# Two-layer decoder trunk on one core: causal mask added by VectorE with the row maximum, ACT issuing the stores of what it wrote, and first scores in single PSUM banks

## Chip, core and metric

The kernel runs on one core of one Trainium2 chip. The metric is the device time of one execution in microseconds (us), less is better. The core has a matrix engine (TensorE, PE in the profile; its weight loads are listed apart as PEld), a vector engine (VectorE, DVE), a scalar engine (ScalarE, ACT), GpSimd (POOL) and SyncE (SP), which here issues most DMA transfers. Each engine works through its own instructions in order and waits on semaphores of the others. Matmuls write to PSUM (eight banks of 2 KB for each of 128 partitions), everything else lives in SBUF.

## The reference

An input of 1024 tokens x 1024 features, all in fp32, passes two layers. Layer 0 is a matrix-memory LSTM (mLSTM) followed by an MLP; then keys and values are computed once from the residual stream; layer 1 is attention with its own low-rank query path, then another MLP. What matters here is layer 1's attention: 8 heads, each with 128 plain and 64 rotated query/key columns, causal.

```python
def causal_mla_attention(q_nope, q_rope, k_nope, k_rope, v):
    ...
    scale = (B_NOPE + B_ROPE) ** -0.5
    ...
        s = (jnp.einsum('bqhd,bkhd->bhqk', qn_b, k_nope)
             + jnp.einsum('bqhd,bkd->bhqk', qr_b, k_rope)).astype(jnp.float32) * scale
        qpos = start + jnp.arange(B_QBLOCK, dtype=jnp.int32)
        s = jnp.where(kpos[None, :] <= qpos[:, None], s, -jnp.inf)
        p = jax.nn.softmax(s, axis=-1)
        return jnp.einsum('bhqk,bkhd->bqhd', p.astype(v.dtype), v)
...
def sqrelu_mlp(h, w1, w2):
    return jnp.square(jax.nn.relu(h @ w1)) @ w2
```

## The kernel before

Every fp32 product is made of three passes over operands that are split into a high and a low part (`mm3`, L255 to L257: high x low, low x high, high x high). ACT casts the high part of a weight tile (L549, L190), DVE subtracts it from the tile to get the low part (L550, L191), and PE multiplies. PSUM is split into three pools: `ps` and `pc` with two buffers of one bank each, `pm` with two buffers of two banks each.

The tokens are worked in two halves of 512. A scheduler places the instructions of each engine by a simulated timeline; `two_streams` hands it dense MLP work together with attention work, so that in both attentions the dense matmuls (L255 to L257) stand between the pieces of attention on PE. The first attention treats the first token half (from about 950 to 1215 us of the profile, while layer 0's MLP of the other half runs), the second attention the second half (about 1565 to 1826 us).

A *unit* of attention is one head and one pair j of query blocks of 128 rows, e = 0 and 1; block i = 2j + e sees (i + 1) x 128 keys, so 128 to 512 in the first attention (j = 0, 1) and 640 to 1024 in the second (j = 2, 3). `scores` makes the scores of a unit: for each group of up to 512 keys `score_mm` runs five matmuls (L1584 to L1587 and L1590), and, in the group that holds the diagonal, a sixth with `identb` as the weights and `maskA` as the moving operand (bf16, 128 x 128; -1e30 above the diagonal), which adds the mask in PSUM (L1589). In the first attention both blocks of a unit share one `pm` buffer, in the second each has one. `softmax` then takes the row maximum on DVE (L1594, negated), multiplies it by SCALE (L1595), lets ACT compute Exp from PSUM into an SBUF tile `raw` with the row's sum beside it (L1596), inverts the sum (L1597) and multiplies by it in place (L1598); for e = 0 POOL clears the last 128 columns (L1600). Later PE transposes the probabilities into `pc` (L1704), ACT and DVE split them (L531, L532), and PE multiplies by the values into `ps`; ACT copies the result out (L1724), and it is stored to `oT` (L1725).

`pm` is also what dense matmuls write to, and L199 (DVE adds a PSUM tile to an SBUF tile) empties it.

In the first attention, `prepare_pair` makes queries, keys and values of two heads; the rotated query `T` is finished on DVE (L1567 to L1570). Keys and values of both token halves go to DRAM (`kd` L1646, `vd` L1652, for each a high and a low part), queries of the second half too (`qd`, `td`), and `loaded_head` reads all four back in the second attention (L1681 to L1689). Other stores that the change touches are a copy of the transposed input (`xt_d`, L615), folded weights (`lw`, L1410, high and low part), and transposed residual blocks (`xr`, L1839). Every one of these is issued on SP's queue, on which weight loads stand too (L236, L212, L376 and others), in one order; a store on it waits until its data are written, and what is behind it waits too. At the start, SP loads the conditioning vector, the input (L317), the first weights (L1926), then eight tiles of `ada_w` (L376, L341), which DVE works through (L381, L383) before the first dense matmuls.

Of the kernel before, what the change touches and what calls it, by code (L numbers as in the profile page):

```python
# [9 lines left out]
F32 = mybir.dt.float32  # L10
# [73 lines left out]
def kernel(  # L84
# [72 lines left out]
    def const(shape, dt, name):  # L157
        return sb.tile(shape, dt, tag=name, bufs=1, name=name)
# [289 lines left out]
    def gate(i, g, s):  # L448
        nc.vector.tensor_mul(mods[:, i], g, s)
        return mods[:, i]  # L450

    identb = const([P, P], BF16, "identb")
    nc.vector.tensor_copy(identb, ident)
    maskA = const([P, P], BF16, "maskA")
    mt = tmp()
    nc.gpsimd.memset(mt[:, :P], 0.0)
    nc.gpsimd.affine_select(
        out=mt[:, :P], in_=mt[:, :P], pattern=[[-1, P]], compare_op=ALU.is_ge,
        fill=-1e30, base=0, channel_multiplier=1,
    )  # L460
    nc.vector.tensor_copy(maskA, mt[:, :P])

    e8 = const([P, NH], F32R, "e8")
    nc.vector.memset(e8.bitcast(F32), 0.0)
    selW = const([P, 4, P], F32R, "selW")
# [142 lines left out]
    def norm0(h, xt, y, A, sh):  # L608
        rstd = along_tokens(tmp(), y)
        for k in range(KD):  # L610
            pt = ps()
            turn(xt[k // 4], pt, k % 4)
            a, u = tmp(), tmc()
            nc.scalar.copy(a, pt)
            nc.sync.dma_start(xt_d[1][ts(k, P)], a)  # L615
            nc.vector.scalar_tensor_tensor(u, pt, A[:, k : k + 1], rstd, ALU.mult, ALU.mult)
            split_mod(h.hi[k], h.lo[k], u, sh[:, k : k + 1])
            yield
# [770 lines left out]
    def latent_weights():  # L1389

        v = wcols(kv_w_a, 256, 64)
        views = [[(0, wcols(kv_w_a, m * P))] for m in range(2)] + [[(0, v), (64, v)]]
        views += [[(0, wcols(b_w_q_a[0], m * P))] for m in range(3)]
        for b, vs in enumerate(views):
            A, sh = (Akv, kvada[:, 0:8]) if b < 3 else (Aq, adac(1, SH1))
            r_ = raw()
            r = r_.rearrange("p (a b) -> p a b", b=P)
            for c0, v in vs:
                nc.sync.dma_start(r[:, :, c0 : c0 + v.shape[2]], v)
            yield  # L1400
            acc = tma()[:, :P]
            with paced():
                nc.vector.tensor_scalar(acc, r[:, 0], sh[:, 0:1], None, ALU.mult)
                for k in range(1, KD):
                    nc.vector.scalar_tensor_tensor(
                        acc, r[:, k], sh[:, k : k + 1], acc, ALU.mult, ALU.add
                    )
            nc.vector.tensor_mul(r, r, A.unsqueeze(2).to_broadcast([P, KD, P]))
            for i, t in enumerate(wsplit(r_, D)):
                nc.sync.dma_start(lw[b, i], t.bitcast(F32))  # L1410
            yield "wait"
            pt = pc()
            nc.tensor.transpose(pt[:, :P], acc, ident)
            nc.vector.reduce_sum(lbias[:, b : b + 1], pt[:, :P], axis=AX.X)
# [3 lines left out]
    def latent(hf, behind):  # L1418

        ready = []

        def load(b):
            with tc.high_priority(PRIO):
                w = []
                for i in range(2):
                    t = raw(F32R)
                    if i == 0:
                        t = sb.tile([P, 1024], F32R, tag="ws", bufs=WS, name=f"lw_{next(uid)}")  # L1430
                    nc.sync.dma_start(t.bitcast(F32), lw[b, i])
                    w.append(t.rearrange("p (a b) -> p a b", b=P))
                ready.append(w)

        load(0)
        load(1)
        yield 0
        h = hf.xn

        def proj(b):  # L1440
            if b < 4:
                load(b + 2)
            w, pt = ready.pop(0), pc() if b == 2 else ps()
            for k in range(KD):
                mm3(pt, w[0][:, k], w[1][:, k], h.hi[k], h.lo[k], k == 0, k == KD - 1)
            return pt

        lb = lambda b: lbias[:, b : b + 1]
        hf.cs = hdv()
        for i in range(2):  # L1450
            nc.sync.dma_start(hf.cs[:, i], rope_d[i][:, ts(hf.i, H)])
        if hf.i:
            hf.kk = [hd(F32R), hd(F32R)]
            for i in range(2):
                nc.sync.dma_start(hf.kk[i][:, 0:H].bitcast(F32), kkd[i])
        else:
            t = hdv(F32R)
            hf.kk = [t[:, 0], t[:, 1]]
        s = ts(hf.i, H)
        ck, cq0, cq1 = k4v(), k4v(), k4v()  # L1460
        cq = [cq0[:, 0], cq0[:, 1], cq1[:, 0]]
        def scaled(o, m):

            pt = proj(m)

            if not rx:
                rx.append(sums_rstd(hf.xx, D, Cst.rearrange("p a b -> p (a b)")[:, :H]))
            nc.vector.tensor_mul(o, pt, rx[0])
            return o

        def based(o, m):
            nc.scalar.activation(o, scaled(o, m), AF.Identity, bias=lb(m))

        rx = []
        for m in range(2):
            based(ck[:, m], m)
        rp = rope(scaled(tmc(), 2), hf, lb(2))
        next(rp)
        yield 0
        rs = rstd_steps([ck[:, 0], ck[:, 1]], 256)  # L1480
        next(rs)
        based(cq[0], 3)
        yield 0
        kr = last_of(rp)
        rstd_k = last_of(rs)
        nc.scalar.copy(hf.kk[0][:, s], kr)
        nc.vector.tensor_sub(hf.kk[1][:, s], kr, hf.kk[0][:, s].bitcast(F32))
        if not hf.i:
            for i in range(2):
                nc.sync.dma_start(kkd[i], hf.kk[i].bitcast(F32))  # L1490
        for m in range(1, 3):
            based(cq[m], 3 + m)
        yield 0
        behind()
        rs = rstd_steps(cq, 384)
        next(rs)
        hi, lo = k4v(F32R), k4v(F32R)
        with paced():
            for m in range(2):
                u = ck[:, m]  # L1500
                nc.vector.scalar_tensor_tensor(u, u, col(KVL + m, 1), rstd_k, ALU.mult, ALU.mult)
                split_mod(hi[:, m], lo[:, m], u, None)
        hf.ckv = ([hi[:, m] for m in range(2)], [lo[:, m] for m in range(2)])
        yield 3 - hf.i
        rstd = last_of(rs)
        yield 0
        ah, al, b = k4v(F32R), k4v(F32R), k4v(F32R)
        his, los = [ah[:, 0], ah[:, 1], b[:, 0]], [al[:, 0], al[:, 1], b[:, 1]]
        for m in range(3):
            u = cq[m]  # L1510
            nc.vector.scalar_tensor_tensor(u, u, col(QL + m, 1), rstd, ALU.mult, ALU.mult)
            split_mod(his[m], los[m], u, None)
        hf.cq = (his, los)
        yield 1
# [58 lines left out]
    def score_mm(o2, kk, q, kn, i):  # L1573
# [5 lines left out]
        for g in range((n + 511) // 512):  # L1579
# [5 lines left out]
            nc.tensor.matmul(o[:, :w], qh, kl, start=False, stop=False)  # L1585
            nc.tensor.matmul(o[:, :w], qT, kk[1][:, ks], start=False, stop=False)
            nc.tensor.matmul(o[:, :w], qT, kk[0][:, ks], start=False, stop=False)  # L1587
            if g == i // 4:
                nc.tensor.matmul(o[:, ts(i % 4, P)], identb, maskA, start=False, stop=False)  # L1589
            nc.tensor.matmul(o[:, :w], qh, kh, start=False, stop=True)  # L1590

    def softmax(f, pr, n, even):
        m, l = small(1), small(1)
        nc.vector.reduce_max(m, f, axis=AX.X, negate=True)  # L1594
        nc.vector.tensor_scalar(m, m, SCALE, None, ALU.mult)  # L1595
        nc.scalar.activation(pr[:, :n], f, AF.Exp, bias=m, scale=SCALE, accum_out=l)  # L1596
        nc.vector.reciprocal(l, l)  # L1597
        nc.vector.tensor_scalar(pr[:, :n], pr[:, :n], l, None, ALU.mult)  # L1598
        if even:
            nc.gpsimd.memset(pr[:, n : n + P], 0.0)  # L1600

    def scores(kk, unit):
# [1 line left out]
        (_, q, kn, _), j = unit  # L1604
        prs = []
        if j < 2:
            st = pm()
            pr = raw().rearrange("p (a b) -> p a b", b=512)
            for e in range(2):
                score_mm(lambda g: st[:, e], kk, q, kn, 2 * j + e)  # L1610
# [20 lines left out]
    def prepare_pair(p_, hf):  # L1631
# [11 lines left out]
        k_half(kn, wkv, hf)  # L1643
        for r in range(2):
            for i in range(2):
                nc.sync.dma_start(kd[2 * p_ + r, i, :, ts(hf.i, H)], kn[r][i].bitcast(F32))  # L1646
        yield 1
        vt = [k4v(F32R, 256) for _ in range(2)]
        v = v_half(wkv, hf, vt)
        for r in range(2):  # L1650
            for i in range(2):
                nc.sync.dma_start(  # L1652
                    vd[2 * p_ + r, i, :, ts(hf.i, H)].rearrange("p (t e) -> p t e", e=P),
                    vt[i][:, :, ts(r, P)].bitcast(F32),
                )
# [37 lines left out]
    def attend(hf, groups, dense, behind=lambda: None):  # L1693
# [18 lines left out]
        def products(work, PT):  # L1712
            n = 0
            for u, b0, nb in work:
# [5 lines left out]
                if b0 + nb == u.nk:  # L1720
                    s = ts(u.j % 2, 256)
                    if u.hh < 6:
                        o = tmp()[:, :256]
                        nc.scalar.copy(o, u.po)  # L1724
                        nc.sync.dma_start(oT[ts(u.hh, P), ts(u.j, 256)], o)  # L1725
                    else:
                        split_mod(hf.o.hi[u.hh][:, s], hf.o.lo[u.hh][:, s], u.po, None)

# [94 lines left out]
    def x_to_rows(half):  # L1823
# [7 lines left out]
        for k in range(KD):  # L1831
# [4 lines left out]
            if k + 1 < KD:  # L1836
                a = get(k + 1)
            nc.scalar.copy(b, pt)
            nc.sync.dma_start(  # L1839
                xr[ts(half, H), ts(k, P)].rearrange("(t p) n -> p t n", p=P),  # L1840
                b.rearrange("p (t n) -> p t n", n=P),
            )
# [330 lines left out]
    drain(p1)  # L2173
    two_streams(with_weight_sums(f0), behind(bg_latent(), 4))
    rope_perm()


    B = {}
# [129 lines left out]
```

## Time and profile before

| what | us |
|---|---|
| median of 3 runs | 2361.49 (2361.12 to 2361.56) |
| the profiled execution | 2359.22 |
| its span, first to last instruction | 2357.3 |
| PE busy in it | 2321.8 (98%) |
| PE weight loads, beside the matmuls | 1959.9 (83%) |
| DVE busy | 1605.7 (68%) |
| ACT busy | 1098.2 (47%) |
| POOL busy | 155.0 (7%) |

The granted PE clock was 0.997 of the full one over the span. How to read the rows: a row of a group gives line, engine, operation, output<-inputs, shapes and count, then total busy us and mean ns of one, then the idle time of the engine just before them with what ended it. A row of the chain of waits gives who waited for whom, then total us, times and longest. A row in order of time gives start and duration in us, then the same names, and in brackets the idle time ahead of it. A row of one source line gives least/median/greatest ns, then first and last start. Buffer numbers are left out of the names. The ends of matmuls are modelled, since they overlap.

### The profile page before, as it was taken

What the parts mean: (1) busy time and instruction counts of PE and PEld (TensorE: products, weight loads), DVE (VectorE), ACT (ScalarE), POOL (GpSimd) and SP (SyncE); (2) the same over time, 40 slices, a digit from 0 to 9 for tenths busy, and PEclk for the clock granted to TensorE, in tenths of its full rate; (3) what the DMA queues carried; (4) which work ended last, traced back from release to release, by engine and by line L of the source; (5) the groups of instructions that cost most, each with busy time, mean ns of one, the idle gap of its engine ahead of it and who ended that gap; (6) DMA issues with size and microseconds to landing.
All of it is one profiled execution on the core that took longest, in us unless ns stands there. A gap on an engine that the chain in (4) does not pass through costs nothing.

```text
span 2357.3 us, 32527 instructions
## 1 busy us (share of the span) xinstructions
PE 2321.8 (98%) x12181; PEld 1959.9 (83%) x12181; DVE 1605.7 (68%) x2657; ACT 1098.2 (47%) x1826; POOL 155.0 (7%) x353
## 2 busy tenths in 40 slices
PE   7999999999999999999999999999999999999998
PEld 5888898888888888888888888888888888989997
DVE  6677876867685777777764967765656488557556
ACT  4355335654343354334444554434444445655543
POOL 1010000000001110111010110010001000000000
PEclk9999999999999999999999999999999999999999
DMA  9452664545566876667764665885544553656562
GB/s 314 144 153 82 191 184 149 156 141 163 174 184 179 284 222 188 184 195 207 211 160 126 199 200 183 274 274 172 163 134 134 143 164 97 185 173 217 166 185 88
DMA packets 408349, 420.76 MB, mean 178 GB/s; under 512 B 27427, under 2 KB 310112, under 8 KB 404608
## 3 DMA queue, kind: packets, MB, share of 16 engines
q1 hardware_dynamic: 402272, 385.02, 52.1%
q0 software_dynamic: 5920, 33.66, 6.5%
q8 instruction: 96, 1.57, 0.3%
q14 instruction: 61, 0.50, 0.1%
HBM read 359.37 MB, written 92.80 MB: 192 GB/s over the span
## 4 chain that ended last, share of the span: by engine, by line
PE 89%; DVE 5%; DMA 4%; ACT 1%; issue 1%; SPq 0%; DVEq 0%; ACTq 0%
PE ps L255 15%; PE ps L257 15%; PE ps L256 15%; PE pm L255 10%; PE pm L256 10%; PE pm L257 10%; DMA raw<-in_mlp_w_dram 2%; PE pc L256 2%; PE pc L257 2%; PE pc L255 2%; PE pc L1704 1%; DMA raw<-in_a_w_in_dram 1%; PE pm L1590 1%; PE pm L899 1%; PE pm L1584 1%
## 5 line engine op out<-in xcount | busy, mean ns | idle before, releaser
L255 PE MATMUL ps<-k,wl 128*128 128x512 f32 (+1 forms) x1432 | 546.3, 381 | 1.6 <-DVE wl L191 1.3
L257 PE MATMUL ps<-k,wh 128*128 128x512 f32 (+1 forms) x1432 | 539.0, 376 | 0.0
L256 PE MATMUL ps<-k,wh 128*128 128x512 f32 (+1 forms) x1432 | 537.4, 375 | 0.0
L549 ACT CAST wh<-raw 128x1024 fp32r<-128x1024 f32 x272 | 285.0, 1051 | 481.4 <-PE ps L255 149.0
L550 DVE TENSOR_TENSOR wl<-raw,wh 128x1024 fp32r<-128x1024 f32 x272 | 331.7, 1221 | 249.4 <-ACT wh L549 155.4
L255 PEld LDWEIGHTS ps<-k,wl 128*128 128x128 f32 x1432 | 269.6, 188 | 53.7 <-issue 3.6
L257 PEld LDWEIGHTS ps<-k,wh 128*128 128x128 f32 x1432 | 269.4, 188 | 50.1 <-issue 0.7
L256 PEld LDWEIGHTS ps<-k,wh 128*128 128x128 f32 x1432 | 269.8, 188 | 48.9 <-issue 1.7
L199 DVE TENSOR_TENSOR k<-k,pm 128x512 f32<-128x512 f32 (+1 forms) x254 | 210.9, 858 | 83.3 <-PE pm L257 82.0
L191 DVE TENSOR_TENSOR wl<-raw,wh 128x1024 fp32r<-128x1024 f32 (+2 forms) x110 | 128.1, 1166 | 115.6 <-ACT wh L190 115.4
L255 PE MATMUL pm<-hd,wl 128*128 128x512 f32 x512 | 201.4, 393 | 0.5 <-ACT hd L531 0.5
L256 PE MATMUL pm<-hd,wh 128*128 128x512 f32 x512 | 199.3, 390 | 0.2 <-DVE hd L532 0.2
L257 PE MATMUL pm<-hd,wh 128*128 128x512 f32 x512 | 199.3, 390 | 0.0
L255 PE MATMUL pm<-wh,hd 128*128 128x512 f32 x488 | 192.2, 394 | 2.9 <-ACT raw L1596 2.5
L256 PE MATMUL pm<-wl,hd 128*128 128x512 f32 x488 | 190.3, 390 | 0.0
L257 PE MATMUL pm<-wh,hd 128*128 128x512 f32 x488 | 190.2, 390 | 0.0
L190 ACT CAST wh<-raw 128x1024 fp32r<-128x1024 f32 (+2 forms) x110 | 109.4, 996 | 172.3 <-PE ps L255 82.9
L1596 ACT ACTIVATE raw<-pm,sm 128x128 f32<-128x128 f32 (+3 forms) x64 | 47.5, 742 | 152.4 <-DVE sm L1595 122.8
L532 DVE TENSOR_TENSOR hd<-tmp,hd 128x512 fp32r<-128x512 f32 x128 | 88.0, 688 | 38.6 <-ACT hd L531 37.9
L255 PEld LDWEIGHTS pm<-hd,wl 128*128 128x128 f32 x512 | 96.2, 188 | 21.0 <-ACT hd L531 0.9
L256 PEld LDWEIGHTS pm<-hd,wh 128*128 128x128 f32 x512 | 96.2, 188 | 20.5 <-DVE hd L532 0.5
L257 PEld LDWEIGHTS pm<-hd,wh 128*128 128x128 f32 x512 | 96.1, 188 | 20.1
(391 smaller groups left out, 4274.9 us busy)
## 6 DMA issues: line engine op xcount, KB each, us to landing
raw<-in_mlp_w_dram SPq DMA_DIRECT2D x240, 512.0 KB, 4.3
raw<-in_ada_w_dram SPq DMA_DIRECT2D x80, 512.0 KB, 4.6
raw<-in_a_w_in_dram SPq DMA_DIRECT2D x48, 512.0 KB, 4.4
sums<-in_mlp_w_dram POOLq DMA_DIRECT2D x96, 256.0 KB, 4.5
raw<-sums SPq DMA_DIRECT2D x64, 256.0 KB, 3.7
xs<-k SPq DMA_DIRECT2D x40, 256.0 KB, 5.6
raw<-in_kv_ada_w_dram SPq DMA_DIRECT2D x16, 512.0 KB, 4.1
raw<-in_a_w_out_dram SPq DMA_DIRECT2D x16, 512.0 KB, 4.9
```

The source lines that it names most:

```text
L190: nc.scalar.copy(hi[:, :n], r[:, :n])
L191: i = nc.vector.tensor_sub(lo[:, :n], r[:, :n], hi[:, :n].bitcast(F32))
L199: return f(*a, **k)
L255: nc.tensor.matmul(o, ll, rh, start=start, stop=False, **m)
L256: nc.tensor.matmul(o, lh, rl, start=False, stop=False, **m)
L257: pe_last[0] = nc.tensor.matmul(o, lh, rh, start=False, stop=stop, **m)
L532: nc.vector.tensor_sub(lo, u, hi.bitcast(F32))
L549: nc.scalar.copy(hi, u)
L550: nc.vector.tensor_sub(lo, u, hi.bitcast(F32))
L899: nc.tensor.matmul(nv[:, r, i], hf.PT[p_][:, r, cs], v[2 * p_ + r], start=g == 0, stop=True,)
L1584: nc.tensor.matmul(o[:, :w], ql, kh, start=True, stop=False)
L1596: nc.scalar.activation(pr[:, :n], f, AF.Exp, bias=m, scale=SCALE, accum_out=l)
```

## The change

The mask matmul goes. Its place takes one DVE instruction (`tensor_tensor_reduce`), which reads the scores in PSUM and a mask `maskw` in SBUF (bf16, 1024 columns, all zero but the last 128), adds them, multiplies by -SCALE, writes the result to the SBUF tile `raw` and gives the minimum over the row; a second, short DVE instruction delivers that minimum. Exp then reads `raw` and writes to it. `maskw` is made once by POOL after the rotary tables, in the tile `Cst` that had held them; a scratch use of `Cst` in `latent` moves to `cq1`. In the first attention, the scores of j = 0 go to a `pc` buffer of one bank instead of a `pm` buffer of two. And 86 stores (8 of L615, 6 of L1410, 16 each of L1646, L1652 and L1839, 24 of L1725) are issued on ACT's queue, those whose data ACT wrote; the low parts, written by DVE, stay on SP. The lines of the changed kernel have lower numbers: scores L1573 to L1577, the new DVE instruction L1581, Exp L1584, inversion L1585, multiplication L1586, copy L1712, store L1713.

```diff
-    identb = const([P, P], BF16, "identb")
...
-    maskA = const([P, P], BF16, "maskA")
...
-            nc.sync.dma_start(xt_d[1][ts(k, P)], a)
+            nc.scalar.dma_start(xt_d[1][ts(k, P)], a)
...
-                nc.sync.dma_start(lw[b, i], t.bitcast(F32))
+                (nc.sync if i else nc.scalar).dma_start(lw[b, i], t.bitcast(F32))
...
-                rx.append(sums_rstd(hf.xx, D, Cst.rearrange("p a b -> p (a b)")[:, :H]))
+                rx.append(sums_rstd(hf.xx, D, cq1[:, 1]))
...
-            if g == i // 4:
-                nc.tensor.matmul(o[:, ts(i % 4, P)], identb, maskA, start=False, stop=False)
             nc.tensor.matmul(o[:, :w], qh, kh, start=False, stop=True)
 
     def softmax(f, pr, n, even):
         m, l = small(1), small(1)
-        nc.vector.reduce_max(m, f, axis=AX.X, negate=True)
-        nc.vector.tensor_scalar(m, m, SCALE, None, ALU.mult)
-        nc.scalar.activation(pr[:, :n], f, AF.Exp, bias=m, scale=SCALE, accum_out=l)
+        nc.vector.tensor_tensor_reduce(
+            pr[:, :n], f, maskw[:, 1024 - n :], -SCALE, 3e38, ALU.add, ALU.min, m
+        )
+        nc.scalar.activation(pr[:, :n], pr[:, :n], AF.Exp, bias=m, scale=-1.0, accum_out=l)
...
-            st = pm()
+            st = pm() if j else pc().rearrange("p (a b) -> p a b", b=256)
...
-                nc.sync.dma_start(kd[2 * p_ + r, i, :, ts(hf.i, H)], kn[r][i].bitcast(F32))
+                (nc.sync if i else nc.scalar).dma_start(kd[2 * p_ + r, i, :, ts(hf.i, H)], kn[r][i].bitcast(F32))
...
-                nc.sync.dma_start(
+                (nc.sync if i else nc.scalar).dma_start(
                     vd[2 * p_ + r, i, :, ts(hf.i, H)].rearrange("p (t e) -> p t e", e=P),
...
-                        nc.sync.dma_start(oT[ts(u.hh, P), ts(u.j, 256)], o)
+                        nc.scalar.dma_start(oT[ts(u.hh, P), ts(u.j, 256)], o)
...
-            nc.sync.dma_start(
+            nc.scalar.dma_start(
                 xr[ts(half, H), ts(k, P)].rearrange("(t p) n -> p t n", p=P),
...
     rope_perm()
+    maskw = Cst.rearrange("p a b -> p (a b)")[:, :H].bitcast(BF16)
+    nc.gpsimd.memset(maskw, 0.0)
+    nc.gpsimd.affine_select(
+        out=maskw[:, 896:], in_=maskw[:, 896:], pattern=[[-1, P]], compare_op=ALU.is_ge,
+        fill=-1e30, base=0, channel_multiplier=1,
+    )
```

At the start, the preparation of `identb` and `maskA` is gone, SP issues the first load of L1926 behind the eight tiles of `ada_w` instead of ahead of them, and DVE makes the low part of those weights (L191) after four instructions of L1920 instead of ahead of L381. Elsewhere the order on PE is the same but for the 64 masks and a few rows.

On PE, the first scores of the second pair of heads in the first attention stood like this, behind the dense matmuls that write `pm` (k are keys and queries, hd the rotated keys):

```order
L257 MATMUL pm_9267<-hd_8805,wh_9074 128x512
L1584 MATMUL pm_9290<-k_1595_9046,k_1616_9166 128x256
L1585 MATMUL pm_9290<-k_1595_9046,k_1616_9166 128x256
L1586 MATMUL pm_9290<-hd_7841,k_1622_9198 128x256
L1587 MATMUL pm_9290<-hd_7841,k_1622_9198 128x256
L1589 LDWEIGHTS identb
L1589 MATMUL pm_9290<-maskA,identb 128x128
L1590 MATMUL pm_9290<-k_1595_9046,k_1616_9166 128x256
```

And now:

```order
L257 MATMUL pm_9246<-hd_8784,wh_9053 128x512
L1573 MATMUL pc_9269<-k_1594_9025,k_1615_9145 128x256
L1574 MATMUL pc_9269<-k_1594_9025,k_1615_9145 128x256
L1575 MATMUL pc_9269<-hd_7836,k_1621_9177 128x256
L1576 MATMUL pc_9269<-hd_7836,k_1621_9177 128x256
L1577 MATMUL pc_9269<-k_1594_9025,k_1615_9145 128x256
```

The mask's two rows are gone, and the scores go to `pc`; their place behind the dense matmuls is the same.

On DVE, the softmax of that head's two blocks followed the read-out of `pm` by L199 (sm are columns of one value for each row):

```order
L199 TENSOR_TENSOR k_1255_7413<-k_1255_7413,pm_9267 128x1024
L1594 TENSOR_REDUCE sm_9304<-pm_9290 128x1
L1595 TENSOR_SCALAR sm_9304<-sm_9304 128x1
L1597 RECIPROCAL sm_9305<-sm_9305 128x1
L1594 TENSOR_REDUCE sm_9312<-pm_9290 128x1
L1598 TENSOR_SCALAR raw_9291<-raw_9291,sm_9305 128x128
L1595 TENSOR_SCALAR sm_9312<-sm_9312 128x1
```

And now:

```order
L199 TENSOR_TENSOR k_1254_7408<-k_1254_7408,pm_9246 128x1024
L1581 ISA raw_9270,sm_9281<-pc_9269,Cst 128x128
L1581 ISA sm_9281 128x1
L1581 ISA raw_9270,sm_9288<-pc_9269,Cst 128x256
L1581 ISA sm_9288 128x1
L1585 RECIPROCAL sm_9282<-sm_9282 128x1
```

The second block's maximum stood behind L1597, which waits for the first block's Exp; now it stands ahead of it.

On ACT, in the second attention, a unit's two Exp were followed by the copy of another head's output (tmp) and the casts of transposed probabilities:

```order
L1596 ACTIVATE raw_14310,sm_14312<-pm_14298,sm_14311 128x896
L1596 ACTIVATE raw_14331,sm_14333<-pm_14319,sm_14332 128x1024
L1724 COPY tmp_14365<-ps_14276 128x256
L531 CAST hd_14368<-pc_14370 128x512
L531 CAST hd_14368<-pc_14377 128x512
```

And now:

```order
L1584 ACTIVATE raw_14236,sm_14238<-raw_14236,sm_14237 128x896
L1584 ACTIVATE raw_14255,sm_14257<-raw_14255,sm_14256 128x1024
L1712 COPY tmp_14288<-ps_14203 128x256
L1713 DMA oT<-tmp_14288 128x256
L520 CAST hd_14291<-pc_14293 128x512
L520 CAST hd_14291<-pc_14300 128x512
```

The store, which stood on SP between two weight loads, is now issued by ACT between the copy and the casts.

More of the change, by code (lines that the diff above doesn't have):

```diff
@@ L450, in gate @@
         return mods[:, i]
-    identb = const([P, P], BF16, "identb")
-    nc.vector.tensor_copy(identb, ident)
-    maskA = const([P, P], BF16, "maskA")
[L455 to L461, printed above, removed]
     e8 = const([P, NH], F32R, "e8")
```

## The prediction

> **What bounds the kernel now.** I read the busy line of the page first, then the chain of work that ended last, then the table by stages for the two stretches where attention runs.
>
> ```profile
> span 2357.3 us, 32527 instructions
> PE 2321.8 (98%) x12181; PEld 1959.9 (83%) x12181; DVE 1605.7 (68%) x2657; ACT 1098.2 (47%) x1826; POOL 155.0 (7%) x353
> PE 89%; DVE 5%; DMA 4%; ACT 1%; issue 1%; SPq 0%; DVEq 0%; ACTq 0%
> 940.00:1230.00 290.00, 285.91 (x1487) 240.66 (x1486) 222.66 (x415) 125.58 (x230) 35.81 (x85) 1.00 0.67 191
> 1550.00:1830.00 280.00, 275.18 (x1533) 234.52 (x1532) 173.49 (x309) 119.00 (x203) 25.78 (x66) 1.00 0.55 170
> ```
>
> TensorE is busy 98% of the span and holds 89% of the chain, so only two things can shorten the run: matmuls that are not issued, and moments in which PE stands still. The last two lines (length, then PE, PEld, DVE, ACT, POOL busy, clock, DMA share, GB/s) are the stages of the first and the second attention: PE stands still 4.1 and 4.8 us in them, DVE is busy 77% and 62%, ACT 43%. The other stages hold no scores. Who lets PE go is in the chain of waits (total, times, longest, in us):
>
> ```profile
> PE pm L1584 <- DVE k L199: 2.9, 4, 0.9
> PE pm L1584 <- DVE sm L1046: 1.2, 3, 0.5
> PEld pm L255 <- ACT raw L1596: 5.2, 7, 1.5
> PE pm L1586 <- DMA k<-td: 1.1, 1, 1.1
> PE pc L1704 <- DVE raw L1598: 0.5, 3, 0.2
> ```
>
> The first two are first scores that wait for a pm buffer which DVE is still reading out, the third dense MLP work that waits for a pm buffer which Exp still reads, the fourth a late load, the fifth the transposes of the probabilities. The next rows are the scores of one head and the start of the next head's, in order of time (start, duration); they price both a mask matmul and a stall.
>
> ```profile
> 1032.67 0.39 PE L256 MATMUL pm<-hd,wh 128*128 128x512 f32 x1
> 1032.90 0.39 PE L257 MATMUL pm<-hd,wh 128*128 128x512 f32 x1
> 1033.74 0.39 PE L1584 MATMUL pm<-k,k 128*128 128x256 f32 x1 [0.45 <-DVE sm L1046]
> 1033.96 0.28 PE L1585 MATMUL pm<-k,k 128*128 128x256 f32 x1
> 1034.20 0.28 PE L1587 MATMUL pm<-hd,k 128*128 128x256 f32 x1
> 1034.32 0.23 PE L1589 MATMUL pm<-maskA,identb 128*128 128x128 bf16 x1
> 1034.36 0.37 PE L1590 MATMUL pm<-k,k 128*128 128x256 f32 x1
> 1034.56 0.27 PE L1584 MATMUL pm<-k,k 128*128 128x256 f32 x1
> ...
> 1035.07 0.36 PE L1590 MATMUL pm<-k,k 128*128 128x256 f32 x1
> 1036.33 0.38 PE L1584 MATMUL pm<-k,k 128*128 128x256 f32 x1 [0.90 <-DVE k L199]
> 1036.55 0.28 PE L1585 MATMUL pm<-k,k 128*128 128x256 f32 x1
> ```
>
> Ends of matmuls are modelled, so I count from start to start: 0.12 us for 256 columns (two from 1033.96 to 1034.20), 0.23 us for 512 (1032.67 to 1032.90).
>
> **Part 1, the mask matmuls go.** From L1587 (1034.20) over the mask to the next score's L1584 (1034.56) pass 0.36 us; two matmuls without a mask would take 0.24. One mask thus costs 0.12 us, and its row here counts them:
>
> ```profile
> L1589 PE MATMUL pm<-maskA,identb 128*128 128x128 bf16 x64 | 14.7, 230 | 0.0
> L1594 DVE TENSOR_REDUCE sm<-pm 128x1 f32<-128x1024 f32 x8 | 9.8, 1223 | 3.4 <-PE pm L1590 3.4
> L199 DVE TENSOR_TENSOR k<-k,pm 128x1024 f32<-128x1024 f32 x50 | 60.7, 1216 | 18.2 <-PE pm L257 18.1
> L1595 DVE TENSOR_SCALAR sm<-sm 128x1 f32<-128x1 f32 x64 | 9.7, 151 | 1.0
> L1596 ACT ACTIVATION_READ_ACCUMULATOR raw<-pm,sm 128x1 f32 x64 | 12.3, 193 | 0.0
> ```
>
> 64 x 0.12 = 7.7 us. The bounds are 64 x 0.04 = 2.6 us (if the 0.20 from 1034.36 to 1034.56 belonged to L1590) and the busy time of 14.7 us, which counts the drain that overlaps the next matmul. I take 7.7, because start to start is what PE's stream loses. Nothing hides it: PE is the bound, and weights for its later matmuls are prepared ahead, since no wait of PE on a weight stands in the list for these stages.
>
> [...]
>
> **Part 2, the fused operation on DVE.** 64 reduces and 64 multiplications by SCALE become 64 operations that add the mask, scale and take the minimum, and 64 reads of the accumulator. No row shows this operation. Nearest are the reduce over the same columns (1223 ns at 1024) and an addition of an SBUF tile and a PSUM tile (L199, 1216 ns): the same price with one or two inputs, so I take the reduce's. The accumulator's read is bounded by L1595 (151 ns) and by ACT's read (193 ns): 64 x 0.04 = 2.7 us on DVE at worst, hidden beside PE, since DVE has 38% and 23% idle in these stages. Exp now reads SBUF instead of PSUM; I cost it at nothing, hidden in ACT's idle 57%. Where that cover is gone are the transposes that wait for L1598 (0.5 us in all by the row above); they grow by what the chain grows.
>
> **Part 3, pm comes free after the fused operation, not after Exp.** The seven waits of dense matmuls (5.2 us on the weight load's row) are this. The worst two follow one another:
>
> ```profile
> 1604.54 0.50 PE L255 MATMUL pm<-wh,hd 128*128 128x512 f32 x1 [0.81 <-ACT raw L1596]
> 1606.39 0.95 DVE L1594 TENSOR_REDUCE sm<-pm 128x1 f32<-128x768 f32 x1
> 1607.17 0.39 PE L257 MATMUL pm<-wh,hd 128*128 128x512 f32 x1
> 1608.68 0.50 PE L255 MATMUL pm<-wh,hd 128*128 128x512 f32 x1 [1.13 <-ACT raw L1596]
> 1609.02 0.39 PE L256 MATMUL pm<-wl,hd 128*128 128x512 f32 x1
> ```
>
> The second loses 1608.68 - 1607.17 - 0.23 = 1.28 us and 0.11 more at the restart (0.34 to the next start): 1.39, for 1.55 idle on the weight load (the longest of the third wait), so the seven lose about 0.9 x 5.2 = 4.7. The first vanishes, since the maximum must be done before Exp, for which PE waits, can start. The second does not vanish whole: what comes late next is DVE, which starts on the second maximum at 1606.39 and would end it about 1607.5, while PE, 1.2 us earlier without the first stall, is there at 1606.2. About 1.3 us stay. Gain 4.7 - 1.3 = 3.4 us, between 2.1 (another such pair) and 4.7.
>
> **Part 4, first scores in single banks (pc).** Of the seven waits the rows give 4.1 us idle. The one at 1033.74 costs 0.84 - 0.23 = 0.61 and 0.10 at the restart, 0.26 more than its idle 0.45; the one at 1036.33 costs 1.14 + 0.10, 0.34 more than 0.90. With 0.3 for each: 4.1 + 2.1 = 6.2 us. What comes late next is the rotated query, and behind it the softmax on DVE:
>
> ```profile
> 1031.14 0.69 DVE L1570 TENSOR_TENSOR k<-tmc,tmp 64x512 fp32r<-64x512 f32 x1
> 1040.86 0.37 DVE L1598 TENSOR_SCALAR raw<-raw,sm 128x256 f32<-128x256 f32 x1
> 1043.36 0.82 PE L1704 MATMUL pc<-ident,raw 128*128 128x128 f32 x6
> ```
>
> The query is done at 1031.83 and PE would want it at 1033.13: 1.3 us in hand. The normalised probabilities are done at 1041.23, 2.1 us before PE transposes them; PE comes 0.71 + 1.24 + 4 x 0.12 = 2.4 us earlier, and DVE, which has its own queue to work off first, may not. So up to 0.3 us of each of four pairs returns as a wait for L1598, unless the two maxima of a head, now one behind the other, start Exp sooner. I take 5.0 of the 6.2, between 2 and 6.2.
>
> **Part 5, 86 stores from SP's queue to ACT's.** Issue times stand in the lines of the stores (ns, least, median, most):
>
> ```profile
> L1725 SPq DMA_DIRECT2D oT<-tmp x24: 320/339/1551, 989.3 to 1770.0; - x24
> L1652 SPq DMA_DIRECT2D vd<-k x32: 360/518/1404, 947.2 to 1554.7; - x32
> 1568.39 0.50 PE L1586 MATMUL pm<-hd,k 128*128 128x512 f32 x1 [1.10 <-DMA k<-td]
> ```
>
> Loads behind a store on SP no longer wait until ACT has written its data, but PE waits for a load only once here: at 1568.39 (1.10 idle, with the 0.3 of part 4 some 1.4 us lost), for a load that SP issues just after four vd stores. Two of those leave: 2 x 0.52 = 1.0 us if SP alone is late; I take half, -0.5, between -1.4 and 0. On ACT each store stands behind the copy that it stores, so it waits for nothing, and delays what follows by 0.34 to 0.52 us: 86 of them are 29 to 45 us of an engine that is idle 1259 us. If every one reached PE, +29; the nearest row is the list of waits, where dense work waits for Exp alone, and that wait goes. I take +0.5, between 0 and +3.
>
> **Part 6, the start.** The mask's preparation leaves the start, and the first weights' load moves behind eight other loads, which land one load earlier:
>
> ```profile
> 12.52 1.22 DVE L191 TENSOR_TENSOR wl<-raw,wh 128x1024 fp32r<-128x1024 f32 x1 [1.22 <-ACT wh L190]
> 20.80 1.54 DVE L383 SCALAR_TENSOR_TENSOR tmc<-k,cond,tmc 128x512 f32<-128x512 f32 x2 [1.17 <-DMA k<-in_ada_w_dram]
> ```
>
> DVE waits for those loads, so its chain comes about 1.35 us earlier (two loads in 1.54 + 1.17 us), but the 1.22 us of L191, done in idle time at 12.52, now stands in the chain: -0.1, between -1.4 and +1.2.
>
> **The sum.** -7.7 - 3.4 - 5.0 - 0.5 + 0.5 - 0.1 = -16.2 us. The profiled execution took 2359.22 us (span 2357.3 and 1.9 around it), 2.3 below the runs' median of 2361.49; so 2343.0 profiled, and 2345 as a median.
>
> **The rivals.** (a) *The fused operation is a slow one.* If it passes over its columns more than once, both maxima of a unit come late on DVE, one behind the other, and PE stands at the transposes. In the second attention 640 to 1024 columns take about 1.0 us on average by the reduce's rate; at 2.5 times that a unit's second half is 2 x 1.5 = 3.0 us late, less what is in hand (between 0, as the transposes' waits show, and the 2.1 us of part 4; 0.8 taken), in 16 units: +35 us, against 16.2 of gains: +19, 2380. It decides from about twice the reduce's time, where 16 x (2.0 - 0.8) = 19 us outweigh the gains. For it speaks that no row shows the operation; against it, that two inputs cost as much as one (1216 against 1223 ns). (b) *Stalls only change their name.* DVE and ACT stay the last in both attentions, by ACT's stores or the softmax chain; of parts 3 and 4 nothing is left: -8, 2353. For it the small reserves (0.8 to 2.1 us), against it ACT's idle time. (c) *The mask was cheap*, 0.04 us: -16.2 + 5.1 = -11.1, 2350. [...] (d) *The change does not do what it says*: PE is held by something that start to start hides, and nothing moves, 2360.
>
> **How the numbers follow.** My forecast 0.63, (a) 0.07, (b) 0.15, (c) 0.10, (d) 0.05. The measurement tells about 0.2% (4.7 us) from no change: forecast, (b) and (c) are faster (0.88), (d) the same, (a) slower. Downwards the range goes to the bounds of all stalls and some of the mask's busy time: 2337. Upwards it takes in (b): 2354. (a) and (d) stay out.
>
> **What the changed profile would show.** Part 1: L1589 gone, 64 matmuls fewer, each score 0.12 us shorter. Part 2: fused operation near 1.22 us at 1024 columns. Part 3: no dense matmul waiting for Exp, one waiting for DVE's maximum. Part 4: no first score behind L199. Part 5: SP's waits for ACT's copies gone, none new on PE. Wrong it is if the fused operation shows 2 us or more, or waits for L1598 add up to several us.

## The result: 2342.4 us, 0.8% faster, and the profile after

| | before | after |
|---|---|---|
| median | 2361.52 us (4 runs) | 2342.44 us (4 runs: 2341.8 to 2344.91) |
| profiled execution, its span | 2359.22, 2357.3 us | 2344.91, 2343.2 us |

The ratio is 0.9919, with a 95% interval of 0.9907 to 0.9931: 16 to 22 us less, 19.1 by the medians. The forecast was 2345, with a range of 2337 to 2354. The profiled execution of the changed kernel is the longest of its four, so what follows rests on a second trace of the same kernel too (e1 below, 2340.57 us).

The page of the changed kernel has these lines, busy time and the chain:

```profile
span 2343.2 us, 32341 instructions
PE 2312.6 (99%) x12117; PEld 1959.8 (84%) x12117; DVE 1599.9 (68%) x2655; ACT 1101.6 (47%) x1826; POOL 156.6 (7%) x353
PE 93%; DMA 3%; DVE 2%; issue 1%; ACT 1%; SPq 0%; DVEq 0%; ACTq 0%
```

PE has 64 instructions and 9.2 us of busy time less; its share of the chain went from 89% to 93%, and DVE's from 5% to 2%. The two stages of attention, in the second trace's table of stretches (length, then PE, PEld, DVE, ACT and POOL busy, granted clock, DMA share, GB/s):

```profile
940.00:1230.00 290.00, 289.33 (x1496) 247.52 (x1495) 224.05 (x419) 130.97 (x233) 36.11 (x86) 1.00 0.69 198
1550.00:1830.00 280.00, 279.23 (x1542) 242.42 (x1541) 173.93 (x312) 124.46 (x208) 29.04 (x65) 1.00 0.58 179
```

PE now stands still 0.7 and 0.8 us in stages in which it stood still 4.1 and 4.8 (2.1 and 0.8 us in the first trace). The groups of the fused operation, of the second trace as well (busy us, mean ns of one, then the idle time ahead of them):

```profile
L1581 DVE CUSTOM_DVE_ANT_0 raw<-pm,Cst 128x1024 f32<-128x1024 f32 x8 | 9.8, 1225 | 3.2 <-PE pm L1577 2.8
L1581 DVE DVE_READ_ACCUMULATOR2_ANT sm<- 128x1 f32 x64 | 5.3, 83 | 0.0
```

The fused operation takes 1225 ns at 1024 columns, as the reduce did (1223), and its accumulator is read in 83 ns. In the chain of waits, of the five rows that the prediction began with, this is left in the second trace, the late load and a rest of the weight loads of the transposes (2.2 us on the same row before):

```profile
PE pm L1575 <- DMA k<-td: 0.8, 1, 0.8
PEld pc L1692 <- DVE raw L1586: 1.0, 6, 0.2
```

And the scores, first head of the second pair, in order of time:

```profile
1031.71 0.39 PE L257 MATMUL pm<-hd,wh 128*128 128x512 f32 x1
1031.94 0.28 PE L1573 MATMUL pc<-k,k 128*128 128x256 f32 x1
...
1032.41 0.28 PE L1577 MATMUL pc<-k,k 128*128 128x256 f32 x1
1032.53 0.28 PE L1573 MATMUL pc<-k,k 128*128 128x256 f32 x1
...
1033.01 0.28 PE L1577 MATMUL pc<-k,k 128*128 128x256 f32 x1
1033.13 0.28 PE L1573 MATMUL pc<-k,k 128*128 128x256 f32 x1
```

They follow the dense matmul after its own 0.23 us, and one another every 0.12 us: neither a mask nor a stall is left, also at the second head (1033.13), which had waited 0.90 us.

SP's waits for data that ACT writes, as the prediction wanted to see, are gone with the stores. In the kernel before, the largest rows of this kind were 44.2 us (L1410) and

```profile
SPq L1725 <- ACT tmp L1724: 34.5, 13, 7.5
```

and neither trace of the changed kernel has such a row for the six kinds of store that moved.

### The profile page after: what moved, and what is told of

The parts are those of the page before. It is cut to its first block, busy times and chain, and to the rows that moved or that the text cites. A ratio compares the mean times of both kernels' runs of the same rounds, so it can differ in the third digit from the quotient of the medians.

```text
span 2343.2 us, 32341 instructions
## 1 busy us (share of the span) xinstructions
PE 2312.6 (99%) x12117; PEld 1959.8 (84%) x12117; DVE 1599.9 (68%) x2655; ACT 1101.6 (47%) x1826; POOL 156.6 (7%) x353
## 4 chain that ended last, share of the span: by engine, by line
PE 93%; DMA 3%; DVE 2%; issue 1%; ACT 1%; SPq 0%; DVEq 0%; ACTq 0%
PE ps L255 16%; PE ps L256 15%; PE ps L257 15%; PE pm L256 10%; PE pm L255 10%; PE pm L257 10%; PE pc L255 2%; PE pc L256 2%; PE pc L257 2%; PE pc L1692 2%; DMA raw<-in_a_w_in_dram 1%; PE pm L1575 1%; PE pm L1576 1%; PE pm L888 1%; PE pm L1577 1%
## 5 line engine op out<-in xcount | busy, mean ns | idle before, releaser
L539 DVE TENSOR_TENSOR wl<-raw,wh 128x1024 fp32r<-128x1024 f32 x272 | 331.3, 1221 | 242.4 <-ACT wh L538 148.3
L199 DVE TENSOR_TENSOR k<-k,pm 128x512 f32<-128x512 f32 (+1 forms) x254 | 210.6, 858 | 83.0 <-PE pm L257 81.9
L191 DVE TENSOR_TENSOR wl<-raw,wh 128x1024 fp32r<-128x1024 f32 (+2 forms) x110 | 127.6, 1163 | 118.2 <-ACT wh L190 118.1
L521 DVE TENSOR_TENSOR hd<-tmp,hd 128x512 fp32r<-128x512 f32 x128 | 87.9, 688 | 41.7 <-ACT hd L520 41.0
L1036 POOL COPY sm<-sm 128x1 f32<-128x1 f32 x128 | 48.6, 388 | 946.1 <-DVE sm L1035 942.6
```

The lines of the kernel that those rows point to most:

```text
L191: i = nc.vector.tensor_sub(lo[:, :n], r[:, :n], hi[:, :n].bitcast(F32))
L199: return f(*a, **k)
L521: nc.vector.tensor_sub(lo, u, hi.bitcast(F32))
L539: nc.vector.tensor_sub(lo, u, hi.bitcast(F32))
L1036: now = nc.gpsimd.tensor_copy(seen, flag)
```

## The experiments

Each kernel was timed in turn with the kernel before; medians are of its own runs, ratios against the kernel before on the same chip. Rows of waits come from one execution each, and that can lie off the median: 4.0 us below it in e5, 2.4 below in e6, 2.1 above in e2. The program also orders the engines' queues anew at each edit, so an experiment can move more than the lines that it edits.

**e1: the changed kernel again.** No edit.

> The changed kernel once more, for a second trace. The profiled execution shown took 2344.91 us and the others about 2342.4; its trace has a stretch of half clock near 268 us (about 1.7 us), waits of PE near 921 to 951 us (about 1.9 us) and one of 1.8 us at 1139 us behind a late load. If these belong to that execution alone, the second trace lacks them and its span is about 2340 to 2341 us; if they are the kernel's own, the waits near 921 to 951 and 1139 us stand in it again and only the half clock is gone. Median 2342.4 either way.

Measured: 2341.36 us, ratio 0.9917 [0.9902, 0.9932]; profiled 2340.57 us. The long wait is not the kernel's own: in the first trace PE waited 1.8 us at 1139 us, here 0.3 us on the same row. It stood behind DVE, which waited for an `ada_w` load, 2.7 us there and 1.2 us at most here. Of the waits near 921 to 951 us a part stands in both: from 915 to 955 us PE stands still 1.0 us in the first trace and not at all in the kernel before; of its three waits there, 0.3 us each, the second trace has two (0.3 us behind L1363, 0.2 behind L539). A dip of the granted clock near 268 us is gone too. The row of that stretch in the first trace (columns as in the stages above, the clock behind the five engines):

```profile
260.00:280.00 20.00, 18.72 (x104) 15.63 (x103) 15.79 (x28) 6.65 (x14) 2.02 (x1) 0.91 0.65 195
```

And in the second:

```profile
260.00:280.00 20.00, 18.75 (x119) 16.17 (x118) 17.02 (x28) 6.67 (x14) 2.04 (x1) 1.00 0.72 219
```

**e2: stores back on SP.**

```diff
-            nc.scalar.dma_start(xt_d[1][ts(k, P)], a)
+            nc.sync.dma_start(xt_d[1][ts(k, P)], a)
```

and so for the other five kinds of store.

> The changed kernel with its 86 stores back on SP's queue; all else as changed. By the prediction the stores are worth nothing (-0.5 for a late load, +0.5 on ACT): 2342.4, within 1 us. The rival, read from the two traces: before, ACT's weight cast at 1599.80 us waited 4.05 us for its load, and the maximum, Exp and PE's wait at 1604.54 us stood behind it; after, that load is early. If stores on SP delay loads in this way, some of the waits of the second attention come back: 2344 to 2347. If the stores on ACT cost more than they bring, 2340 to 2341.5.

Measured: 2345.67 us, ratio 0.9934 [0.9922, 0.9947], 4.3 us above e1 and 3.2 above the changed kernel's first median. The rival's size was right, its place was not: no wait for Exp came back. Three rows of the chain of waits in e2:

```profile
PE ps L256 <- DVE hd L521: 2.2, 2, 1.9
PE pm L1575 <- DMA k<-td: 1.7, 1, 1.7
PE pm L255 <- DVE sm L1035: 1.1, 1, 1.1
```

PE waits 0.9 us longer for the td load than in either trace of the changed kernel (1.7 against 0.8), and 1.1 us behind L1035 (a marker of one column that DVE writes) against 0.3 and nothing. The 2.2 us behind L521, however, can't be put down to the stores. Their main part, one wait of 1.9 us, stands on the row on which the first trace of the changed kernel has its wait at 1139 us, with the stores on ACT:

```profile
PE ps L256 <- DVE hd L521: 1.8, 1, 1.8
```

The engines that use the loaded tiles say no more. What ACT and DVE waited for in the first attention (900 to 1230 us), e2:

```profile
ACT wh L538 <- DMA raw<-in_mlp_w_dram: 28.7, 15, 4.0
DVE tma L383 <- DMA raw<-in_ada_w_dram: 4.6, 3, 2.8
```

e1, with the stores on ACT's queue:

```profile
ACT wh L538 <- DMA raw<-in_mlp_w_dram: 25.4, 16, 3.5
DVE tma L383 <- DMA raw<-in_ada_w_dram: 1.7, 2, 1.2
```

In the first trace of the changed kernel, with the stores on ACT as well, the same row of DVE has 3.8 us (three waits, the longest 2.7 us). So DVE's longer wait comes and goes between executions of one kernel. That the stores cost the changed kernel 3.2 to 4.3 us on SP is measured; by which loads they do it, beyond that of td, is not shown.

**e3: mask matmuls back on PE.** The fused operation stays, with a mask of zeros.

```diff
+            if g == i // 4:
+                nc.tensor.matmul(o[:, ts(i % 4, P)], identb, maskA, start=False, stop=False)
```

> The changed kernel with the 64 mask matmuls put back on PE; DVE's fused operation stays, with a mask of zeros. The prediction's price of 0.12 us each: 2342.4 + 7.7 = 2350. The rival of a cheap mask (0.04 us): 2345. [...] If the scores' 4 more matmuls also move a wait, up to 1 us beside.

Measured: 2351.06 us, ratio 0.9955 [0.9943, 0.9968]; 9.7 us above e1 of the same chip, 8.6 above the changed kernel's first median. That is 0.13 to 0.15 us for each mask, somewhat above the prediction's 0.12, and far above 0.04. In proportion to a score's 0.12 us for 256 columns, the mask's 128 columns would be an estimated 0.06 us, and the mask costs at least twice that. The rows of the kernel before bear out the prediction's price at every width: from the mask's start to the start behind the score that follows it pass 0.24, 0.30 and 0.36 us at 256, 384 and 512 columns (at 1034.32, 979.98 and 981.21 us), against 0.12, 0.18 and 0.23 us for such a score alone. That is 7.7 to 8.3 us in all; of the rest, the load of td explains 0.6 us (PE waited 1.4 us for it, 0.8 in e1).

**e4: as e3, Exp from PSUM again.**

```diff
-        nc.scalar.activation(pr[:, :n], pr[:, :n], AF.Exp, bias=m, scale=-1.0, accum_out=l)
+        nc.scalar.activation(pr[:, :n], f, AF.Exp, bias=m, scale=SCALE, accum_out=l)
```

> As e3 (mask matmuls on PE, fused operation with a mask of zeros), but Exp reads the scores from PSUM again, so that pm is held until Exp is done; the difference to e3 is what the earlier release of pm is worth. The prediction: 3.4 us more than e3 (2353.4 if e3 takes 2350). By the trace after, in which all seven waits for Exp are gone: 5 us more. Rival: the waits came from late loads ahead of the maximum, and stay gone: as e3, within 1 us.

Measured: 2350.82 us, ratio 0.9957 [0.9945, 0.997], the same as e3 (2351.06). Exp holds pm again, and still PE hardly waits for it; of 5.2 us on the weight load's row there is left:

```profile
PEld pm L255 <- ACT raw L1588: 1.5, 4, 0.7
```

So the earlier release of pm, to which the prediction gave 3.4 us, is worth nothing that this measurement can tell, once the rest of the change is in.

**e5: the kernel before, stores on ACT.** The edit is e2's, the other way.

> The kernel before with the 86 stores on ACT's queue and nothing else changed. By the prediction worth nothing: 2361.4, within 1 us. By e2 (stores back on SP cost the changed kernel some 3.9 us): 2357.5. If the seven waits for Exp of the second attention came from weight loads that stood behind stores on SP, they go too: 2353 to 2355, and the row of PE's weight loads that wait for Exp (5.2 us, 7 times) is gone from its trace.

Measured: 2359.04 us, ratio 0.9989 [0.998, 0.9998]: 2.5 us less. The two rows that tell the theories apart:

```profile
PEld pm L255 <- ACT raw L1596: 5.6, 7, 1.5
PE pm L1584 <- DVE k L199: 1.3, 2, 0.9
```

The seven waits for Exp stay whole (5.6 us), so they do not come from stores on SP. First scores, however, wait for a pm buffer 1.3 us, all of it behind L199, where it was 4.1 us behind L199 and L1046 (the marker of one column in the kernel before, which ends with L199 in these rows). The stage of the first attention shows it too: PE stands still 1.4 us there instead of 4.1, and 4.9 instead of 4.8 us in the second. ACT also waits less for its loads in this trace: over the same 900 to 1230 us, its cast of the MLP weights waited 19.4 us in the kernel before,

```profile
ACT wh L549 <- DMA raw<-in_mlp_w_dram: 19.4, 10, 3.9
```

and in e5

```profile
ACT wh L549 <- DMA raw<-in_mlp_w_dram: 11.9, 7, 3.3
```

That a load which stands behind fewer waiting stores comes earlier, and that DVE gets to the read-out of pm earlier for that reason, fits these rows but is not shown by them: in the two traces of the changed kernel, with the stores on ACT as well, this row of ACT is 24.1 and 25.4 us, more than the 19.4 of the kernel before with all of them on SP.

**e6: the fused operation alone.** e4 with the stores on SP and the first scores in pm.

> The fused operation alone: mask matmuls on PE (fused operation with a mask of zeros), Exp from PSUM, first scores in pm, stores on SP; only the start is that of the changed kernel. e4 showed that the waits for Exp are gone even while Exp holds pm. If the shorter chain on DVE (one operation and a short read for a reduce and a multiplication) does that by itself: 5 us for them and 1 to 2 us for the transposes that wait for L1598, 2354 to 2356. If the stores do it (loads earlier): only the transposes' 1 to 2 us, 2360. The prediction costs the fused operation at nothing: 2361.4.

Measured: 2356.53 us, ratio 0.9978 [0.997, 0.9987]: 5.0 us less. Mask on PE, Exp from PSUM, and the two waits are almost gone:

```profile
PEld pm L255 <- ACT raw L1588: 1.2, 4, 0.4
PEld pc L1696 <- DVE raw L1590: 0.2, 1, 0.2
```

How, one unit shows, from the start of the maximum to the start of Exp. In the kernel before, in order of time:

```profile
1599.80 1.05 ACT L549 CAST wh<-raw 128x1024 fp32r<-128x1024 f32 x1 [4.05 <-DMA raw<-in_mlp_w_dram]
...
1602.03 0.82 DVE L1594 TENSOR_REDUCE sm<-pm 128x1 f32<-128x640 f32 x1
...
1602.76 0.68 DVE L532 TENSOR_TENSOR hd<-tmp,hd 128x512 fp32r<-128x512 f32 x1
1603.36 0.15 DVE L1595 TENSOR_SCALAR sm<-sm 128x1 f32<-128x1 f32 x1
1603.60 0.80 ACT L1596 ACTIVATE raw<-pm,sm 128x640 f32<-128x640 f32 x1 [0.94 <-DVE sm L1595]
```

The same unit in e6:

```profile
1598.54 1.05 ACT L540 CAST wh<-raw 128x1024 fp32r<-128x1024 f32 x1 [2.72 <-DMA raw<-in_mlp_w_dram]
...
1600.76 0.82 DVE L1585 CUSTOM_DVE_ANT_0 raw<-pm,Cst 128x640 f32<-128x640 f32 x1
1601.50 0.08 DVE L1585 DVE_READ_ACCUMULATOR2_ANT sm<- 128x1 f32 x1
...
1601.68 0.80 ACT L1588 ACTIVATE raw<-pm,sm 128x640 f32<-128x640 f32 x1 [0.28 <-DVE sm L1585]
```

Before, another operation of 0.68 us stood on DVE between the maximum and its multiplication by SCALE, and Exp began 1.57 us after the maximum did; now the read follows at once, and Exp begins after 0.92 us. Besides, the weight load ahead of all this landed earlier (ACT waited 2.72 instead of 4.05 us): on SP, e6 like the changed kernel has it ahead of the 512 KB load of td, the kernel before behind it. Before:

```profile
1590.67 0.42 SPq L1686 DMA_DIRECT2D k<-td  x1
1591.20 0.38 SPq L236 DMA_DIRECT2D raw<-in_mlp_w_dram  x1
```

In e6:

```profile
1591.02 0.38 SPq L236 DMA_DIRECT2D raw<-in_mlp_w_dram  x1
1591.46 1.07 SPq L1678 DMA_DIRECT2D k<-td  x1
```

The two differences come together in the runs: the weight load goes first in e6 and in both traces of the changed kernel, which have the fused operation, and td's load in the kernel before and in e5 and e9, which keep the maximum. e9 and e10 try to part them.

**e7: first scores in pm again.**

```diff
-            st = pm() if j else pc().rearrange("p (a b) -> p a b", b=256)
+            st = pm()
```

> The changed kernel with the first scores in pm again. The prediction: 5.0 us slower than the changed kernel (2341.4 to 2342.4), 2347, with the seven waits behind L199 back; 6.2 us if the gain was whole (2348); 3 to 4 us (2345) if PE, coming earlier, loses part of it again to late loads.

Measured: 2347.33 us, ratio 0.9942 [0.993, 0.9954]: 4.9 us above the changed kernel's first median and 6.0 above e1's. Four of the seven waits are back:

```profile
PE pm L1573 <- DVE k L199: 2.1, 4, 1.0
```

With 0.3 us more for each, as in the prediction, they explain some 3.3 us; the rest of the difference is not in this row.

**e8: only the start.** In the kernel before, the mask's constants are made after the rotary tables.

> The kernel before, but the mask's constants are made after the rotary tables, so that the start is that of the changed kernel (first weights' load behind the eight ada_w tiles, its low part later on DVE). The prediction: -0.1 us, 2361.3, bounds 2360 to 2362.6. The trace after has PE through its first 41 us 0.3 us earlier: 2361.1.

Measured: 2361.34 us, ratio 1.0003 [0.9993, 1.0012]: nothing, as predicted. The waits of PE at the start are others all the same. The kernel before has 2.9 us behind DVE (L381) and 1.7 us for an `ada_w` load; the changed kernel, with the changed start, has its longest single wait of PE, 4.4 us behind ACT (L523) until 27.7 us, and 1.0 and 0.6 us for an `ada_w` load in its two traces, and e6, with that start too, has 3.9 and 0.7 us on these rows.

**e9: no multiplication.** SCALE is left out of the softmax altogether.

```diff
-        nc.vector.tensor_scalar(m, m, SCALE, None, ALU.mult)
-        nc.scalar.activation(pr[:, :n], f, AF.Exp, bias=m, scale=SCALE, accum_out=l)
+        nc.scalar.activation(pr[:, :n], f, AF.Exp, bias=m, scale=1.0, accum_out=l)
```

> The kernel before without the 64 multiplications by SCALE on DVE (L1595) and with a scale of 1 in Exp; so SCALE is left out of the softmax, and nothing else is changed: reduce, mask on PE, Exp from PSUM, stores on SP, SP's order with td ahead of the weight load. e6 (the fused operation alone) took 5.0 us less than before and had no wait for Exp. If that comes from the chain on DVE (in before another operation of 0.68 us stands between the reduce and the multiplication at 1602.8 us, so that Exp starts late): 2356 to 2357, waits for Exp under 1 us. If it comes from SP's order, in which e6 has the weight load ahead of td's: 2360 to 2361, waits for Exp 4 to 5 us.

Measured: 2358.15 us against 2360.46 for the kernel before, ratio 0.9992 [0.9984, 1.0001]. As a time it is unclear; the trace says between the two:

```profile
PEld pm L255 <- ACT raw L1595: 3.4, 6, 1.2
PEld pc L1703 <- DVE raw L1597: 0.8, 5, 0.2
PE ps L256 <- DVE hd L532: 1.0, 3, 0.3
```

The shorter chain takes a third off the waits for Exp (5.2 to 3.4) and most of the transposes' (2.2 to 0.8 on the same kind of row), and a wait of another kind appears with the new order on DVE. First scores wait for a pm buffer 0.9 us, twice, instead of 4.1 us in seven, although no store was moved. The unit shown under e6 parts the two differences here, for td's load still goes first and the weight load is as late as before:

```profile
1600.31 1.05 ACT L549 CAST wh<-raw 128x1024 fp32r<-128x1024 f32 x1 [4.22 <-DMA raw<-in_mlp_w_dram]
...
1602.53 0.82 DVE L1594 TENSOR_REDUCE sm<-pm 128x1 f32<-128x640 f32 x1
...
1603.44 0.79 ACT L1595 ACTIVATE raw<-pm,sm 128x640 f32<-128x640 f32 x1 [0.27 <-DVE sm L1594]
```

Exp begins 0.91 us after the maximum does, as soon as in e6 (0.92), and yet 3.4 us of the waits for Exp stay. So the shorter chain alone is not what takes them all.

**e10: td loaded through ACT's queue.**

```diff
-            nc.sync.dma_start(flat(held[p_]), td[p_])
+            nc.scalar.dma_start(flat(held[p_]), td[p_])
```

> The kernel before with the four loads of td issued by ACT, so that they no longer stand ahead of the weight loads on SP's queue; nothing else is changed. If SP's order makes the waits for Exp: 2357 to 2358, and ACT's wait for a weight load ahead of the wait at 1604 us falls from 4.05 us to 2.7 us. If the chain on DVE makes them: 2361, within 1 us, and the seven waits for Exp stay at 4 to 5 us.

Measured: 2361.06 us against 2360.46, ratio 1.0006 [0.9998, 1.0015]: no gain. But it does not decide, for the weight load did not land earlier; ACT still waited for it:

```profile
1599.87 1.05 ACT L549 CAST wh<-raw 128x1024 fp32r<-128x1024 f32 x1 [3.74 <-DMA raw<-in_mlp_w_dram]
```

With td's load gone from SP's queue the weight load was issued at 1590.77 us, 0.43 us earlier than in the kernel before, and ACT's cast began no earlier (1599.87 against 1599.80 us). What stays open is how the rest of e6's gain divides between td standing behind the weight load and the order on DVE; an order of SP's queue alone, with all else as before, was not tried.

## Why the prediction was right, term by term

The sum was right: 16.2 us forecast, 19.1 measured (20.1 in e1). Its terms were not all of the right size, and one had the wrong mechanism. That the sum came out so near is in part luck: part 3's 3.4 us came to nothing for the reason given, while parts 2 and 5, put at nothing, brought 5.0 and 2.5 to 4.3 us.

- Part 1, masks, 7.7 us: 8.6 to 9.7 us in e3, of which the rows from start to start give 7.7 to 8.3 to the masks themselves. The reading from start to start, against both the busy time of 14.7 and the 0.04 us, holds; rival (c) falls, and so does (d), that nothing moves.
- Part 2, the fused operation at no cost and no gain: its duration was right (1225 against 1223 ns), so rival (a) falls. But the step "64 reduces and 64 multiplications become 64 operations and 64 reads" was priced by busy time alone. The read (83 ns) lies below the bounds taken (151 and 193 ns), and in the first trace of the changed kernel each of the 64 follows its operation with nothing between, while the multiplication could have another operation ahead of it (0.68 us in the unit shown under e6). The term was put at nothing; e6 measures 5.0 us for the fused operation together with the new place of td on SP's queue, a moved step that the prediction did not price. How the 5.0 us divide is open.
- Part 3, pm free earlier, 3.4 us: the waits for Exp went, all of them, but not for that reason (e4 equals e3, e6 has Exp on PSUM). The step that failed is the attribution of a wait to the resource that is released last: Exp was late because its maximum and the multiplication behind it were. The 1.3 us that were to stay at 1608.68 went too: the chain, which I held fixed, came earlier (the second maximum, at 1606.39 us before, starts at 1604.46 us in e6).
- Part 4, first scores in single banks, 5.0 us: 4.9 to 6.0 (e7). The next in line, query and softmax, did not get late: the second trace has no wait of PE there, and the weight loads of the transposes wait 1.0 us instead of 2.2.
- Part 5, the stores, 0: mis-sized. They are worth 2.5 us alone (e5) and 3.2 to 4.3 us in the changed kernel (e2). The prediction saw one late load of td, and that part is there (0.9 us in e2). The gain of e5, however, lies in the first attention, where waits behind L199 go; the prediction had no term for that, and through which loads it comes is not shown. On ACT the stores cost nothing that shows: PE's wait behind ACT's casts is 0.5 us before and in both traces after (`pm`, L531 and L520).
- Part 6, the start, -0.1: nothing (e8).

The parts overlap: measured one by one (9, 5, 0, 5.5, 3.5, 0) they make some 23 us, of which 19 to 20 arrive. Stores and single banks both take the waits of first scores for a pm buffer (e5 cuts them from seven to two, as e9 does without moving a store; e7's return is four). Rival (b), that stalls only change their name, is refuted by the stage rows: PE stands still 1.4 us in both stages together in the second trace and 2.9 in the first, before 8.9.

## What to carry to other kernels

When PE waits for a late consumer, follow the chain back to what made it late before pricing an earlier release: here the earlier release was worth nothing that shows (e4), while 5.0 us went with a rewrite of the chain ahead of Exp (e6). A rewrite that fuses two dependent operations should be priced by what can come between them on that engine's queue, and its new order looked up on every queue, DMA included. For stores that wait for their data, look at what stands behind them on their queue: here 86 of them, moved from SP's queue with its weight loads to ACT's, were worth 2.5 us alone (e5) and 3.2 to 4.3 us in the changed kernel (e2). And before a wait is explained by an edit, look for it in every trace of the unedited kernel: the longest wait of PE in e2's attention stages stood in one of them already.

## What the runs showed of the hardware that was not expected

The fused operation of two inputs with a scaled output and a row minimum cost on DVE what the reduce cost (1225 and 1223 ns at 1024 columns), and the read of its accumulator 83 ns, a little over half of a one-column multiplication (151 ns). Exp in place on an SBUF tile took a little longer than from PSUM at 1024 columns, 1154 against 1120 ns by the groups of the two kernels. Before:

```profile
L1596 ACT ACTIVATE raw<-pm,sm 128x1024 f32<-128x1024 f32 x8 | 9.0, 1120 | 15.6 <-DVE sm L1595 8.0 <-DVE sm L1046 7.6
```

After, in the first trace:

```profile
L1584 ACT ACTIVATE raw<-raw,sm 128x1024 f32<-128x1024 f32 x8 | 9.2, 1154 | 13.6 <-DVE sm L1581 6.8 <-DVE sm L1035 6.7
```

And one execution lost clock for a moment in the middle of dense work (granted 0.91 from 260 to 280 us in one trace, 1.00 in the other). Two traces of the same kernel stood 4.3 us apart; the clock and the later load at 1139 us are two differences seen between them, and the rest was not traced.
